# First mixer: the order of projections, attention heads, convolution taps and gates in the row of work behind the delta rule

## The chip, the cores and the metric

The kernel runs on one core of a Trainium2 chip. The metric is the time of one execution on the device, in microseconds (us). A trace comes from one profiled execution: its span runs from the first instruction to the last.

## What is computed

Two blocks stand one behind the other. The first has two layers, each a hybrid mixer and a feed-forward part; the second is other code that the change does not touch. For the change only the hybrid mixer matters. 256 tokens of width 1024 are projected once, and three branches share the result:

```python
def hybrid_mixer(x, w_in, mix_scale, w_out, ...):
    proj = jnp.einsum('btd,de->bte', x, w_in)
    (a_q, a_k, a_v, a_decay, a_beta, a_gate, c_glu, f_q, f_k, f_v, f_forget) = split_columns(proj, IN_SIZES)
    ...
    o_a = gated_delta_rule(heads(a_q, GDN_HEADS), heads(a_k, GDN_HEADS), heads(a_v, GDN_HEADS), log_decay, beta)
    o_a = (rms_norm_f32(o_a, gdn_norm_w) * jax.nn.silu(heads(a_gate, GDN_HEADS))).reshape(B, T, GDN_WIDTH)

    glu_a, glu_b = jnp.split(c_glu, 2, axis=-1)
    u = glu_a * jax.nn.sigmoid(glu_b)
    u = causal_depthwise_conv(u, cnv_dw_w) + cnv_dw_b          # 31 taps, 256 channels
    o_b = jax.nn.silu(layer_norm(u, cnv_ln_g, cnv_ln_b))

    log_f = jax.nn.log_sigmoid(f_forget + fox_f_bias)
    o_c = forgetting_attention(heads(f_q, FOX_HEADS), heads(f_k, FOX_HEADS), heads(f_v, FOX_HEADS), log_f)   # 6 heads

    mixed = jnp.concatenate([o_a, o_b, o_c], axis=-1) * mix_scale
    return jnp.einsum('bte,ed->btd', mixed, w_out)
```

All weights and activations are 32-bit floats.

## The kernel before, in words

Activations lie with the channels on the 128 partitions and the 256 tokens along the free axis. Weights come as one stream in the order of their use, in chunks of up to 1 MB ([128, 2048]) through four buffers `raw` (`load_chunk`, line 384). A projection takes its weights in one of two ways, set per group by `WHOLE` (line 165): with 'p' ScalarE and VectorE split each 1024 columns into a high and a low part (`hi`, `lo`, four buffers of each) and TensorE makes three matmuls per 128 x 128 piece (`mm3`); with 'w' one 32-bit matmul is made straight from `raw`, which shows as two records. A weight group accumulates in one PSUM bank of the tag `mm`, of which there are three.

`_mixer1` (line 727) is called once for each of the two layers. Its projections form one generator, `parts` (line 809), one step per call of `next`: the attention's values and the small columns, the delta rule's values v, then fq and fk of the attention (six steps, 'p'), gb and ga of the convolution (four steps each, 'w'), and the gates (two steps 'p', two steps 'w'). `fox` (line 1191) is the attention as a generator of ten steps: one that prepares the decay rows, then for each of three pairs of heads two steps of scores and softmax and one of the product with v. `conv_taps` (line 1166) is the convolution: a first step that starts both channel halves, then 30 steps of two VectorE instructions, `cvacc<-uu,cdwh,cvacc`, one behind the other in each half. It needs `uu`, which is made when ga is complete. `mem_load` (line 1600) loads the second block's memory and scales it by eight ScalarE instructions, and each `mem_units` (line 1610) makes a quarter of one layer's memory keys and values, 32 records of matmuls from a chunk of its own.

The delta rule (`gdn`, line 928) is a long chain of small matmuls and VectorE, ScalarE and GpSimd steps. Behind it `_mixer1` calls `fill(REST)` (line 871), which runs a row of such steps as a string spells it: c is a projection step, x a step of the attention, a digit that many steps of taps, U the memory load and u a memory unit. Steps that are asked for when a generator is at its end do nothing. Behind the row come the split of the attention's output into `mh`, `ml` (which take the buffers of the layer's input `xh`, `xl`, and so wait for the last 'p' projection), the convolution's layer norm (`conv_norm`, line 1179: squares, statistics on TensorE, the norm), one Silu over all gates (`G`), the gating and norm of the delta rule's output (`gdn_out`, line 1143), and the output projection w_out, which takes the attention's rows first, then the convolution's, then the delta rule's (`order = [5, 6, 7, 3, 4, 0, 1, 2]`, line 883 on).

The program's place is a priority and not yet the order of issue. When the program is built, a scheduler fills each engine's queue: of the instructions that its own clockwork holds ready it takes the one that stands first in the program, so work of the row goes into the gaps of the delta rule. Buffers of one tag are given out in the program's order. On the chip each queue runs in its order.

Of the kernel before, what the change touches and what calls it, by code (L numbers as in the profile page):

```python
# [160 lines left out]
FREE = 1  # L161
PRE = 2
FILL = ({'s': 'cccc', 'g': 'cccccc'}, {'s': 'cccc', 'g': 'cccccc'})
REST = 'ccccxccxcxcxcxcxcxcxcccx33x33U333c3c3c3cu999u'
WHOLE = ('wwwpppwwpw', 'pwwpppwwpw')
PG = 2
MO = 6
# [13 lines left out]
class K:  # L181
# [545 lines left out]
    def _mixer1(self, l, first):  # L727
# [94 lines left out]
        def fill(p):  # L822
            for n in p:
                if n == 'c':
                    next(stream, None)
                elif n == 'x':
                    next(box['fox'], None)
                elif n == 'U':
                    self.mem_load(f"m{l}")
                elif n == 'u':  # L830
                    if units:
                        self.mem_units(f"m{l}", [units.pop(0)])
                else:
                    for _ in range(int(n)):
                        next(conv, None)
# [34 lines left out]
        oS = self.gdn(l, qkv, lr, g, lnb, fill)  # L870
        fill(REST)
        mh, ml = self.new_hl()
# [1114 lines left out]
```

## Time and profile before

| | us |
|---|---|
| median of 3 runs | 2951.46 |
| lowest and highest | 2949.2 and 2954.4 |
| the profiled execution | 2954.75 |
| its span | 2952.9 |
| mean granted TensorE clock in it | 0.983 |

The profile's page gives each engine's busy time and groups the instructions by line. Since helpers record every operation (lines 202 to 217), a group is told by its tiles: `out<-in` names what an instruction writes and reads. In the trace layer 0's mixer is at 0 to 230 us and layer 1's at 420 to 640 us. gb and ga are `ps_mm<-x,raw`, taps are `cvacc<-uu,cdwh,cvacc`, the heads' scores are `ps_mm<-cr,selt`, `ps_mm<-selt,cr` and `ps_mm<-fb`, w_out and 'p' projections are `ps_mm<-xh,hi`, `xl,hi`, `xh,lo`, memory units are `ps_mm<-raw`. Matmuls are pipelined, so a busy TensorE need not be at its peak, and the start to start distance in a dense stream is its pace.

### The profile page before, as it was taken

The numbers are of one execution on the slowest core, as the hardware profiler recorded it, in microseconds if no ns is written. First come the engines' busy times: TensorE is split into PE (matmuls) and PEld (weight loads), VectorE is DVE, ScalarE is ACT, GpSimd is POOL, SyncE is SP. The second block draws the span as 40 slices with busy tenths as digits, with TensorE's granted clock in tenths as the row PEclk, the third lists the DMA queues.
The fourth block names the chain that finished last, engine by engine and source line by source line (L and its number), as shares of the span: only waits on it lengthen the run. The fifth ranks groups of instructions, "written<-read, shape, count | busy, mean of one in ns | idle before, by whom it ended". The sixth has DMA issues, their size and how long they took to land.

```text
span 2952.9 us, 48784 instructions
## 1 busy us (share of the span) xinstructions
PE 2894.1 (98%) x19525; PEld 2628.7 (89%) x19525; DVE 2155.8 (73%) x3156; ACT 1754.5 (59%) x2582; POOL 79.8 (3%) x142
## 2 busy tenths in 40 slices
PE   8999999999999999999999999999999999999998
PEld 7889998887888887788878899989999999999998
DVE  6476566479989888988889866676766665867764
ACT  5335445258787777778777744565554444655543
POOL 1100002000000000000000000100000000100000
PEclk9899999899999999999999999999999999999999
DMA  6035542158989997998999755534655555335553
GB/s 226 22 136 186 188 151 99 38 225 350 345 339 358 362 359 296 361 353 331 357 368 357 275 175 188 177 108 158 211 188 192 184 191 193 137 110 194 203 189 112
DMA packets 104205, 663.77 MB, mean 225 GB/s; under 512 B 11808, under 2 KB 17952, under 8 KB 28576
## 3 DMA queue, kind: packets, MB, share of 16 engines
q1 hardware_dynamic: 101664, 658.46, 60.6%
q8 instruction: 156, 2.56, 0.3%
q10 hardware_dynamic: 2304, 2.10, 0.2%
q14 instruction: 81, 0.66, 0.1%
HBM read 657.36 MB, written 3.15 MB: 224 GB/s over the span
## 4 chain that ended last, share of the span: by engine, by line
PE 57%; DVE 2%; ACT 1%; issue 0%; POOL 0%; POOLq 0%; DVEq 0%; ACTq 0%
PE ps_mm L217 47%; PE py L217 5%; PE ps_fx L217 2%; PE ps_sm L217 2%; DVE lo L206 1%; PE ps_fx L227 0%; PE ps_sm L227 0%; DVE aa L1784 0%; ACT hi L202 0%; DVE gi L206 0%; PE ps_st L217 0%; DVE aa L206 0%; ACT xr L203 0%; DVE y L214 0%; DVE ffab L206 0%
## 5 line engine op out<-in xcount | busy, mean ns | idle before, releaser
L206 DVE TENSOR_TENSOR lo<-raw,hi 128x1024 fp32r<-128x1024 f32 (+2 forms) x1216 | 1434.3, 1207 | 384.2 <-ACT hi L202 371.8
L202 ACT ACTIVATE hi<-raw 128x1024 fp32r<-128x1024 f32 (+2 forms) x1216 | 1246.8, 1044 | 622.0 <-PE ps_mm L217 466.7
L217 PE MATMUL ps_mm<-xh,hi 128*128 128x256 f32 x2736 | 777.1, 285 | 13.1 <-ACT hi L202 8.1
L217 PE MATMUL ps_mm<-xh,lo 128*128 128x256 f32 x2736 | 770.2, 282 | 2.1 <-DVE lo L206 2.1
L217 PE MATMUL ps_mm<-xl,hi 128*128 128x256 f32 x2736 | 771.8, 282 | 0.3 <-DVE xl L206 0.3
L217 PEld LDWEIGHTS ps_mm<-xh,hi 128*128 128x128 f32 x2736 | 519.5, 190 | 19.7 <-ACT hi L202 8.8
L217 PEld LDWEIGHTS ps_mm<-xh,lo 128*128 128x128 f32 x2736 | 518.6, 190 | 5.7 <-issue 2.7
L217 PEld LDWEIGHTS ps_mm<-xl,hi 128*128 128x128 f32 x2736 | 520.5, 190 | 3.5 <-issue 2.0
L217 PE MATMUL ps_mm<-lo,xgh 128*128 128x512 f32 x896 | 356.5, 398 | 0.7
L217 PE MATMUL ps_mm<-hi,xgl 128*128 128x512 f32 x896 | 349.8, 391 | 0.0
L217 PE MATMUL ps_mm<-hi,xgh 128*128 128x512 f32 x896 | 349.6, 392 | 0.0
L217 PE MATMUL ps_mm<-ffl,hi 128*128 128x256 f32 x880 | 245.6, 279 | 0.0
L217 PE MATMUL ps_mm<-ffh,hi 128*128 128x256 f32 x880 | 245.6, 279 | 0.0
L217 PE MATMUL ps_mm<-ffh,lo 128*128 128x256 f32 x880 | 245.5, 279 | 0.0
L217 PEld LDWEIGHTS ps_mm<-lo,xgh 128*128 128x128 f32 x896 | 168.4, 188 | 48.4 <-DVE lo L206 16.3
L217 PEld LDWEIGHTS ps_mm<-hi,xgh 128*128 128x128 f32 x896 | 168.5, 188 | 35.6 <-ACT hi L202 0.2
L217 PEld LDWEIGHTS ps_mm<-hi,xgl 128*128 128x128 f32 x896 | 168.6, 188 | 32.5
L217 PE MATMUL py<-lo,hh 128*128 128x512 f32 x448 | 178.5, 398 | 0.5
L217 PE MATMUL py<-hi,hl 128*128 128x512 f32 x448 | 174.8, 392 | 0.5
L217 PEld LDWEIGHTS ps_mm<-ffl,hi 128*128 128x128 f32 x880 | 165.4, 188 | 0.0
L217 PEld LDWEIGHTS ps_mm<-ffh,lo 128*128 128x128 f32 x880 | 165.4, 188 | 0.0
L217 PEld LDWEIGHTS ps_mm<-ffh,hi 128*128 128x128 f32 x880 | 165.4, 188 | 0.0
(433 smaller groups left out, 3735.7 us busy)
## 6 DMA issues: line engine op xcount, KB each, us to landing
raw<-in_sm SPq DMA_DIRECT2D x336, 1024.0 KB, 6.9
raw<-in_s SPq DMA_DIRECT2D x248, 1024.0 KB, 4.8
raw<-in_s SPq DMA_DIRECT2D x40, 512.0 KB, 3.3
raw<-in_s SPq DMA_DIRECT2D x32, 256.0 KB, 2.9
raw<-in_mem SPq DMA_DIRECT2D x5, 1024.0 KB, 4.9
kv<-kvt ACTq DMA_DIRECT2D x16, 128.0 KB, 5.4
raw<-kv SPq DMA_DIRECT2D x16, 128.0 KB, 2.8
raw<-in_s SPq DMA_DIRECT2D x2, 1005.0 KB, 6.7
```

The source lines that it names most:

```text
L202: return self.nc.scalar.activation(out, in_, func, scale=scale, **kw)
L206: return self.nc.vector.tensor_tensor(out=out, in0=a, in1=b, op=op)
L217: return self.nc.tensor.matmul(out, lhsT=l, rhs=r, start=start, stop=stop, skip_group_check=True, **kw)
```

## The change

One string is replaced; no step is added or left out (the last digits of both strings ask for more taps than are left).

```diff
-REST = 'ccccxccxcxcxcxcxcxcxcccx33x33U333c3c3c3cu999u'
+REST = 'ccccccxcccccccc3x3x3x3Ux3ux3x3x3x3xcccc3u9'
```

Written out, with H0 to H5 for the scores of the six heads, PV0 to PV2 for the products with v and tN for the taps up to step N (31 is the last):

```text
before: fq fq fq/fk fq/fk prep fk fk H0 gb H1 gb PV0 gb H2 gb H3 ga PV1 ga H4 ga ga gate
        H5 t3 t6 PV2 t9 t12 U t15 t18 t21 gate t24 gate t27 gate t30 - u t31 u
after:  fq fq fq/fk fq/fk fk fk prep gb gb gb gb ga ga ga ga t3 H0 t6 H1 t9 PV0 t12 U
        H2 t15 u H3 t18 PV1 t21 H4 t24 H5 t27 PV2 gate gate gate gate t30 u t31
```

The row is the same for both layers. The order in which weights stand in the stream follows the order of the loads.

## Rows read from the trace of the kernel before

**Rows 1.** the page, busy times: engine, us, share of the span, instructions
```profile
PE 2894.1 (98%) x19525; PEld 2628.7 (89%) x19525; DVE 2155.8 (73%) x3156; ACT 1754.5 (59%) x2582; POOL 79.8 (3%) x142
```

**Rows 2.** windows: length; busy us of PE, PEld, DVE, ACT, POOL; clock; DMA
```profile
84.00:126.00 42.00, 41.65 (x235) 35.12 (x235) 15.64 (x37) 13.42 (x42) 3.29 (x2) 0.80 0.00 1
126.00:157.00 31.00, 31.00 (x235) 24.39 (x234) 8.83 (x32) 11.22 (x32) 0.00 (x0) 1.00 0.10 35
157.00:184.00 27.00, 27.00 (x157) 23.77 (x155) 26.91 (x73) 8.39 (x18) 0.00 (x0) 1.00 0.39 127
```

**Rows 3.** windows of tile x, PE alone (gb, ga): length, busy us (records), clock
```profile
84.00:126.00 42.00, 10.19 (x26) 0.80 0.00 1
126.00:157.00 31.00, 10.31 (x38) 1.00 0.10 35
...
494.00:530.00 36.00, 6.98 (x24) 0.70 0.00 0
530.00:574.00 44.00, 12.19 (x40) 0.90 0.07 25
```

**Rows 4.** timeline of VectorE, layer 0: start us, us, instruction, idle before
```profile
156.81 0.75 DVE L214 SCALAR_TENSOR_TENSOR uu<-fb,ps_mm 128x256 f32<-128x256 f32 x2 [1.56 <-PE ps_mm L217]
...
164.06 18.17 DVE L214 SCALAR_TENSOR_TENSOR cvacc<-uu,cdwh,cvacc 128x249 f32<-128x249 f32 x48
...
186.72 1.23 DVE L206 TENSOR_TENSOR lo<-raw,hi 128x1024 fp32r<-128x1024 f32 x1
...
198.64 0.88 DVE L214 SCALAR_TENSOR_TENSOR xl<-G,pc,xh 128x256 fp32r<-128x256 f32 x2
```

**Rows 5.** lines of PE in 157 to 184: busy us, mean ns
```profile
L217 PE MATMUL ps_mm<-raw 128*128 128x256 f32 x64 | 14.0, 379 | 0.0
```

**Rows 6.** windows behind the taps, both layers, columns as in rows 2
```profile
184.00:217.50 33.50, 31.26 (x251) 29.74 (x250) 22.70 (x48) 14.76 (x25) 3.35 (x3) 0.95 0.52 197
601.00:627.00 26.00, 24.09 (x207) 23.05 (x206) 16.79 (x32) 14.21 (x23) 4.25 (x3) 1.00 0.64 237
```

**Rows 7.** timeline of PE, layer 0, columns as in rows 4
```profile
192.04 0.28 PE L217 MATMUL ps_mm<-xh,hi 128*128 128x256 f32 x1
...
193.34 0.28 PE L217 MATMUL ps_mm<-xh,lo 128*128 128x256 f32 x1
193.64 1.14 PE L217 MATMUL ps_sm<-cst,ovr 128*64 128x128 f32 x12
```

**Rows 8.** lines of PE in 84 to 126: busy us, mean ns
```profile
L217 PE MATMUL ps_mm<-fb 64*128 64x128 f32 (+1 forms) x12 | 3.5, 375 | 0.0
...
L217 PE MATMUL ps_mm<-cr,selt 128*128 128x256 f32 x6 | 2.2, 364 | 0.0
```

**Rows 9.** timeline of ScalarE, layer 0, columns as in rows 4
```profile
182.22 2.00 ACT L202 ACTIVATE hi<-raw 128x1024 fp32r<-128x1024 f32 x2 [4.16 <-DMA raw<-in_s]
184.13 0.40 ACT L203 ACTIVATE sq<-cvacc 128x256 f32<-128x256 f32 x1
...
195.25 1.28 ACT L203 ACT_TABLE_LOAD   x1
196.54 1.27 ACT L203 ACTIVATE G<-G 128x1280 f32<-128x1280 f32 x1
```

**Rows 10.** loads: the page's DMA group, and the timeline of SP and ScalarE
```profile
raw<-in_s SPq DMA_DIRECT2D x248, 1024.0 KB, 4.8
...
66.00 0.33 SPq L1605 DMA_DIRECT2D raw<-in_mem  x1
...
72.44 2.50 ACT L202 ACTIVATE raw<-raw,pc 128x256 f32<-128x256 f32 x6
```

**Rows 11.** windows: the half clock of layer 1; equal work of both layers
```profile
508.26:538.98 30.72, 30.72 (x129) 27.18 (x130) 6.40 (x13) 7.46 (x21) 1.64 (x1) 0.50 0.00 1
...
84.20:156.80 72.60, 72.25 (x465) 59.12 (x464) 24.07 (x67) 24.63 (x74) 3.29 (x2) 0.88 0.05 16
493.50:574.10 80.60, 80.60 (x468) 66.20 (x467) 26.28 (x76) 24.61 (x74) 5.31 (x5) 0.81 0.04 14
```

## What the change should do to the time: the prediction

> **What bounds the kernel now.** I read the page's busy times first, then the two mixers cut into stretches, then three queues in order of time. The page has TensorE at 2894.1 of 2952.9 us [rows 1], so nothing is won by making another engine faster, only by giving TensorE less to wait for or a better clock. The first mixer runs twice, once per layer. In layer 0 the delta rule runs to about 151 us (its last state product is evicted at 150.07), and TensorE is full in all of 84 to 184 us [rows 2]: the scheduler orders by place in the program but lets whatever is ready go ahead, so the pieces of the row REST already sit in the delta rule's gaps. What TensorE does there is fixed work. The change can't remove it; it can only shorten what comes after, or alter the clock under it.
>
> The place where the order matters is the convolution. Its two projections (gb, ga) are 64 matmul records per layer. In layer 0, 26 fall before 126 us and 38 in 126 to 157; in layer 1, 24 before 530 and 40 by 574 [rows 3]. The last lets `uu` start at 156.81, and the taps then fill VectorE: 48 of them take 18.17 us, 0.379 each, up to 182 us [rows 4]; VectorE is busy 26.91 of 27 us in that stretch [rows 2]. All that time TensorE still has work, 14.0 us of it the two units of memory keys and values [rows 5]. So the taps are late, but TensorE comes to the output projection (w_out) only at 184 us: the taps end about when it does. What is lost stands behind: 184 to 217.5 us holds 251 matmuls in 33.5 us, and in layer 1 601 to 627 holds 207 in 26 us [rows 6]. The pace of w_out at the full clock is 11 steps from 192.04 to 193.34, 0.118 us each [rows 7]. 251 and 207 at that pace are 29.6 and 24.4 us, so 3.9 and 1.6 us are lost, 5.5 together. The 59 and 63 of these that are not w_out's are small and go faster: twelve of them take 1.14 us at 193.64 [rows 7], 0.095 each, which makes 1.4 us more lost in each layer, 8.3 in all.
>
> **The change, part by part.** Nothing is added or taken away: 18 projection steps, 10 attention steps, 31 tap steps, the memory load U and its two units stay, each with the same instructions. Four things move.
>
> (1) gb and ga ahead of the heads. In the gaps before 126 us the heads now take score matmuls of 3.5 and 2.2 us [rows 8], products of 2.4 us and three smaller kinds of 1.6, 1.4 and 1.4 us (the same view); 12.5 us in all. At the 10.19 us that 26 records took there [rows 3], 0.39 each, they hold 32 more. So 58 of 64 are done by 126 and all by about 130 us; in layer 1, by the same count, about 532 instead of 574. TensorE's total is unchanged: 0. Bounds: the same records cost 0.39 there and 0.27 later (10.31 us for 38), but the heads leave that slow stretch in exchange, so I put plus or minus 2 us per layer for the exchange.
>
> (2) Taps between the heads. They start at about 130, need 62 x 0.379 = 23.5 us of VectorE, which in 126 to 157 is busy 8.83 of 31 us [rows 2], and so end near 164 instead of 182. What they meet is the delta rule's own VectorE steps between 126 and 150 (four gram products, three of `qg`, three of `vn`, three groups for the state: 13), each held up by at most one tap, 0.38 us: 0 to 5 us per layer on that chain. TensorE waits for it only if it has nothing else; heads and the first memory unit are ready there. I count 0.5 per layer, 1 us in all, 10 at the upper end.
>
> (3) What is late next. The convolution's statistics stand behind the whole row, and the second memory unit is in the row, so TensorE still takes them up only when the row is empty, near 183 us. So the chain does not move up by 18 us. It gets shorter. Now ScalarE does two weight splits from 182.22 before it squares the taps' sums, the first at 184.13 [rows 9], the second at 185.49 behind a memory unit's eviction; with taps done at 164 both squares are ready, which takes about 1.5 us out. VectorE puts splits of 1.23 us between the steps of the layer norm (186.72 and another behind it) [rows 4]: in layer 0 2.4 us, in layer 1 nothing. From the first statistics at 183.6 to the end of the second operand of the convolution at 199.5 is 15.9 us now; 12.0 then. What TensorE has to put under it is w_out of the attention's three rows, 54 matmuls at 0.118 (6.4 us), and 59 small ones (5.6 us): 12.0. It just covers. So layer 0 keeps about 0.5 of its 3.9 to 5.3 us and layer 1 about 0.5 of its 1.6 to 3.0: a gain of 4.5 to 7.3. I take 6.5, near the end that prices small matmuls by their own pace. Bounds: 0 if the cover fails by the same amount as now, 8.3 if all is recovered.
>
> (4) The gates go last, and the loads go in another order. U and the first unit now stand ahead of the gates, so the four buffers hold gb, ga, memory, unit; the gates' chunk waits for gb's buffer (about 105 us) instead of landing before U, which now issues at 66.00 [rows 10]. A chunk lands 4.8 us after its issue [rows 10] and its two splits take 2 x (1.00 + 1.23) us [rows 4, 9]; it is needed after the heads, behind 150, so I count 0, and 9.3 us per layer if that cover were gone. U's eight scalings (0.42 us each [rows 10], 3.3 us of ScalarE) move forward beside the first decay; the projections' dense stream covers them: 0, or 3.3. The gates' last result must pass table load and Silu (1.28 + 1.27 us [rows 9]), gating and split, about 7.4 us; the second unit (7 us) and w_out's first 6.4 us lie over it: 0.
>
> Sum: -6.5 + 1 and, for the clock, -0.5 (below): -6. Against the profiled execution (2954.75 us, of which 2952.9 is span) that is 2948.7; the median of the runs lies 3.3 us below that execution, so 2945.5 there, which I round to 2945.
>
> **The clock.** TensorE was granted 0.50 (1.2 of 2.4 GHz) in 508.26 to 538.98, with no idle time in it. Nearly the same work (84.20 to 156.80 and 493.50 to 574.10) took 72.6 and 80.6 us at 0.88 and 0.81 [rows 11]. With only 1.0 and 0.5 granted, 0.88 over 72.6 us is 17 us of half clock, so layer 1 had 13.6 us more of it and took 8.0 us longer: 0.6 us per us. In these stretches TensorE was busy with the inverse's small matmuls and one filling item between them. The change swaps those items, attention for projections, and the stretch can come out longer or shorter; I see no reason for a sign beyond layer 1's being the longer, and count -0.5, with -8 to +16 as ends (layer 1 like layer 0; each layer one more stretch of 13.6).
> The Trainium skill, "TensorE: Matmul & The Clock Gate", section "HAM oscillation — how this bites in real kernels", puts the lower clock down to gaps in which TensorE is idle. By that, an order that leaves it no gaps costs and gains nothing in clock, and the third and fourth case below would have no chance. The stretch with 30.72 busy of 30.72 at 0.50 speaks against it here.
>
> **The rivals.**
> A (0.46): as summed, 2942 to 2948, two thirds of it below 2945.6.
> B (0.23): the tail doesn't shorten. The statistics still wait for the row, the splits of w_out's weights still fall into the layer norm's steps (their buffers come free late, with the gates behind), and the gates' Silu takes the taps' place. For it: in layer 1 no split sits between the norm's steps and 1.6 us are lost even so. Against it: the squares no longer wait. Price 0 to 2: 2949 to 2953.
> C (0.15): slower. The projections are used up at about 130, so the rest of the delta rule has only heads and one unit as filling, and the half clock comes back or lasts: from one more 13.6 us in each layer on, 16 us less the 6: 2961; with one of them 2953. It decides once the half clock of the two mixers exceeds its present 48 us by more than 20.
> D (0.16): faster still. More matmuls of 256 columns early end the half clock sooner; layer 1 like layer 0 gives 8 on top of 6: 2937, and 2932 with layer 0 shorter too.
> That the scheduler gives much the same order as before is the lower end of B; the moved buffers speak against it.
>
> **How the numbers follow.** A measurement of this kernel tells 0.2%, 5.9 us, from no change. Faster: two thirds of A and D, 0.46. Same: the rest of A and B, 0.39. Slower: C, 0.15. The range 2932 to 2957 leaves out some of D's lower end and the greater part of C.
>
> **What would show it.** In the new profile: gb and ga complete by about 130 and 532 us; taps end by 165 and 580; the convolution's squares stand directly behind them; the stretch from the first statistics to w_out's end is 4 to 5 us shorter in layer 0 and about 2 in layer 1; TensorE stays full from 84 to 184. Wrong would be: holes in TensorE between 130 and 184, statistics later than 184, or a half clock of other length that outweighs the tail.

## The result and the profile after

The changed kernel takes 2973.5 us (median of 5, 2966.6 to 2974.2) against 2951.5 before: a ratio of 1.0068 [1.0054, 1.0083], slower by some 20 us. The profiled execution spans 2972.0 us at a mean granted clock of 0.979; before, 2952.9 at 0.983.

Executions of one and the same kernel, on one chip, differ by up to 27 us here, and go with the mean granted clock: over all timed executions of this study one line with a common slope, 2.66 us for each 0.001 of clock, leaves a spread of only 1.6 us. So below each kernel has two numbers: its mean clock (uncertain by about 0.0007 for 12 executions), and how far it lies above the kernel before **at equal clock** (about 0.5 us).

The stretches of layer 0 after, in windows (columns as in [rows 2]: stretch, its length, busy us of PE, its weight loads, DVE, ACT and POOL, granted clock, DMA share, GB/s). The first is one stretch of half clock, the next three answer to [rows 2], the last runs from the first statistics to the end of the output projection [rows 6]:

```profile
91.35:122.07 30.72, 30.72 (x124) 27.41 (x124) 5.29 (x8) 7.98 (x24) 1.64 (x1) 0.50 0.04 7
84.00:126.00 42.00, 41.97 (x201) 37.00 (x199) 9.86 (x18) 11.44 (x35) 3.28 (x2) 0.63 0.07 25
126.00:157.00 31.00, 29.96 (x213) 22.63 (x213) 14.66 (x40) 8.93 (x21) 0.00 (x0) 0.99 0.16 52
157.00:184.00 27.00, 27.00 (x159) 22.13 (x157) 21.95 (x69) 11.36 (x35) 0.00 (x0) 0.95 0.15 49
...
194.29:228.56 34.27, 30.26 (x254) 28.72 (x253) 20.75 (x46) 14.60 (x24) 3.35 (x3) 1.00 0.45 164
```

TensorE is as full as before, but at 0.63 in the first 42 us, and it comes to the statistics at 194.29 instead of 183.58. The last row is no shorter than before [rows 6]: 4.0 of 34.27 us without work.

The records of the convolution's projections, which answer to [rows 3]:

```profile
84.00:126.00 42.00, 15.71 (x38) 0.63 0.07 25
126.00:144.40 18.40, 7.45 (x26) 1.00 0.10 30
```

64 records, the last at 144.4. VectorE's timeline around the taps (start, duration, instruction, count; before: [rows 4]) shows `uu` at once behind them and the last taps at 187, not at 164:

```profile
144.38 0.75 DVE L214 SCALAR_TENSOR_TENSOR uu<-fb,ps_mm 128x256 f32<-128x256 f32 x2
145.05 0.41 DVE L211 TENSOR_SCALAR cvacc<-uu,cdwh,pc 128x256 f32<-128x256 f32 x1
...
185.78 1.18 DVE L214 SCALAR_TENSOR_TENSOR cvacc<-uu,cdwh,cvacc 128x227 f32<-128x227 f32 x3
```

ScalarE behind the taps, which answers to [rows 9]:

```profile
187.87 0.41 ACT L203 ACTIVATE sq<-cvacc 128x256 f32<-128x256 f32 x1
192.53 2.01 ACT L202 ACTIVATE hi<-raw 128x1024 fp32r<-128x1024 f32 x2 [4.26 <-DMA raw<-in_s]
194.50 0.39 ACT L202 ACTIVATE kvt<-ps_mm 128x256 f32<-128x256 f32 x1
...
195.57 0.41 ACT L203 ACTIVATE zq<-cvacc 128x256 f32<-128x256 f32 x1
...
201.39 1.06 ACT L202 ACTIVATE hi<-raw 128x1024 fp32r<-128x1024 f32 x1 [5.41 <-PE ps_mm L217]
```

The first square is directly behind the taps, but the second stands behind two weight splits that wait 4.26 us for their load, and behind the eviction of the second memory unit.

In layer 1 the half clock of the inverse is shorter than before (20.48 against 30.72 us [rows 11]), and the tail lies partly at half clock:

```profile
524.84:545.32 20.48, 20.48 (x84) 18.36 (x82) 4.02 (x6) 6.12 (x18) 0.00 (x0) 0.50 0.15 51
614.72:644.81 30.09, 26.79 (x207) 25.68 (x206) 16.31 (x32) 13.35 (x21) 4.26 (x3) 0.89 0.56 206
```

At the end of the output projection the changed kernel is 11.2 us late in layer 0 and 17.8 in layer 1. Of the 6.6 us between, 2.8 arise near 370 us, where TensorE has a stretch of half clock that the kernel before did not have and the code is unchanged; so layer 1's own mixer adds little in this execution.

### The profile page after: what moved, and what is told of

Read it like the earlier page. It is cut to its first block, busy times and chain, and to the rows that moved or that the text cites. A ratio compares the mean times of both kernels' runs of the same rounds, so it can differ in the third digit from the quotient of the medians.

```text
span 2972.0 us, 48789 instructions
## 1 busy us (share of the span) xinstructions
PE 2907.3 (98%) x19525; PEld 2637.2 (89%) x19525; DVE 2154.6 (72%) x3156; ACT 1753.6 (59%) x2582; POOL 76.3 (3%) x142
## 4 chain that ended last, share of the span: by engine, by line
PE 57%; DVE 2%; ACT 1%; issue 0%; POOL 0%; POOLq 0%; DVEq 0%; ACTq 0%
PE ps_mm L217 47%; PE py L217 5%; PE ps_fx L217 2%; PE ps_sm L217 2%; DVE lo L206 1%; PE ps_fx L227 0%; PE ps_sm L227 0%; DVE aa L1784 0%; ACT hi L202 0%; DVE gi L206 0%; PE ps_st L217 0%; DVE aa L206 0%; ACT xr L203 0%; DVE y L214 0%; DVE ffab L206 0%
## 5 line engine op out<-in xcount | busy, mean ns | idle before, releaser
L217 PEld LDWEIGHTS ps_mm<-hi,xgl 128*128 128x128 f32 x896 | 168.8, 188 | 32.5
```

Source lines behind the costliest of these rows:

```text
L217: return self.nc.tensor.matmul(out, lhsT=l, rhs=r, start=start, stop=stop, skip_group_check=True, **kw)
```

## The experiments

All runs at a glance. The medians of the kernel before in the four batches were 2956.5, 2951.5, 2952.9 and 2954.1, its mean clock over 124 executions 0.9839 (0.9830, 0.9848, 0.9840 and 0.9838 in the batches of e1 to e4, of a2 and e5 to e7, of e8 to e11, and of e12 to e15). Behind a run stand 12 executions, but 11 behind a2_after, 9 behind e12_tiny, 6 behind e10 and e11, and 5 behind the first.

| run | median us | ratio to before | mean clock | at equal clock, us |
|---|---|---|---|---|
| changed kernel, first | 2973.5 | 1.0068 [1.0054, 1.0083] | 0.9798 | +7.5 |
| a2_after (the same again) | 2973.7 | 1.0061 [1.0038, 1.0083] | 0.9803 | +8.2 |
| e1_layer0 | 2963.5 | 1.0032 [1.0015, 1.0049] | 0.9814 | +4.4 |
| e2_layer1 | 2955.4 | 1.0004 [0.9988, 1.0021] | 0.9843 | +3.6 |
| e3_taps_behind | 2958.4 | 1.0010 [0.9994, 1.0027] | 0.9846 | +6.5 |
| e4_heads_front | 2954.5 | 0.9988 [0.9964, 1.0012] | 0.9856 | +3.8 |
| e11_units_old | 2978.9 | 1.0083 [1.0051, 1.0114] | 0.9808 | +15.2 |
| e5_unit_behind | 2962.2 | 1.0036 [1.0016, 1.0056] | 0.9825 | +4.2 |
| e7_old_unit_behind | 2957.8 | 1.0019 [0.9997, 1.0040] | 0.9834 | +1.7 |
| e12_tiny (new row, 16 x 16 columns) | 2968.3 | 1.0048 [1.0029, 1.0066] | 0.9826 | +10.4 |
| e13_cols256 (new row, 16 x 256) | 2954.1 | 1.0001 [0.9985, 1.0018] | 0.9879 | +11.1 |
| e6_dense (new row, 16 x 512) | 2953.0 | 1.0004 [0.9990, 1.0019] | 0.9892 | +13.5 |
| e15_old_tiny (old row, 16 x 16) | 2970.6 | 1.0051 [1.0033, 1.0069] | 0.9788 | +2.8 |
| e14_old_cols256 (old row, 16 x 256) | 2947.1 | 0.9974 [0.9960, 0.9988] | 0.9885 | +5.7 |
| e8_old_dense16 (old row, 16 x 512) | 2950.3 | 0.9993 [0.9976, 1.0010] | 0.9872 | +5.6 |
| e9_old_dense8 (old row, 8 x 512) | 2955.4 | 0.9998 [0.9979, 1.0017] | 0.9857 | +4.9 |
| e10_old_dense4 (old row, 4 x 512) | 2985.4 | 1.0103 [1.0075, 1.0130] | 0.9752 | +5.7 |

**Is the lower clock the change's?** The changed kernel was run again beside others.

> The changed kernel once more, beside the others of its batch. The executions of one kernel spread by about 25 us, and go with the mean granted clock of the execution at about 2.65 us for each 0.001. Theory P (part and part): the change costs 7 to 8 us at equal clock, and the other 12 of the first comparison were a lower clock in its five executions (0.980 against 0.983 to 0.986); if that was chance, its mean clock is now like that of the kernel before, and it stands 6 to 10 us above it. Rival K: the longer half clock belongs to the new order; then its mean clock is again 0.003 or more below that of the kernel before and it stands 15 to 20 us above.

Eleven executions, 2956.5 to 2978.8 at 0.986 to 0.977, mean clock 0.9803: K's case. So about 8 us are there at equal clock, and 0.0038 of clock, times 2.66 us for each 0.001, is 10: together the 18 us by which the mean of all 16 executions lies above that of the kernel before (the medians differ by 20 to 22). What one stretch of half clock costs is seen where two executions run the same 134 matmuls of layer 0's inverse, first in a2_after, then in e1_layer0 (windows, columns as above):

```profile
88.12:116.65 28.53, 28.53 (x134) 26.77 (x134) 3.92 (x6) 5.40 (x14) 3.27 (x2) 0.56 0.00 1
```
```profile
87.89:105.41 17.52, 17.52 (x134) 15.91 (x134) 3.92 (x6) 5.21 (x14) 3.28 (x2) 1.00 0.00 1
```

At 0.56, 25.1 of the 28.53 us are half clock; they cost 11.0 us, 0.44 each. The common slope says the same: 0.001 of mean clock over 2954 us is 5.9 us of half clock, and 2.66 over 5.9 is 0.45 (an estimate). The order of instructions alone doesn't decide it: TensorE's order up to the end of layer 0's mixer is the same in these two executions, and ran once at half, once at full clock. What the order shifts is the mean.

**Layer by layer.** The old and the new row as two strings, one per layer:

```
-        fill(REST)
+        fill(REST[l])          # e1: (new, old), e2: (old, new)
```

> The new row in layer 0 alone, the old row in layer 1. Theory K (clock): what the change costs comes mostly from the longer half clock in layer 0's delta rule (34 us of it against 17) and from what it does to the granted clock afterwards; so layer 0 ends its mixer 9 to 12 us later than in the kernel before, and the whole is 2961 to 2967. Rival O (order): each layer loses alike because heads and taps stand in one another's way, about 10 us per layer; then also about 2961, but the loss shows in a stretch at the full clock, between 145 and 195 us, and the layer 1 kernel of this batch loses as much.

> The old row in layer 0, the new row in layer 1 alone. Theory K: in the changed kernel layer 1 had 20.5 us of half clock in the delta rule against 30.7 and won 5 us there, lost some 3 in the row and 4 in the tail; alone it gives 2949 to 2955, and the time goes with the half clock of its own trace at 0.5 us per us. Rival O: each layer loses about 10 us by its order; 2961.

At equal clock +4.4 and +3.6 add up to the +8 of both: each layer loses alike, though not the 10 us that O gave it. The lower clock goes with layer 0, as K had it: beside 0.9830 for the kernel before in the same batch, the new row there alone has 0.9814, in layer 1 alone 0.9843. But -0.0016 and +0.0014 do not add up to the -0.0038 of both, so it isn't shown that layer 0 alone brings the loss of clock. (The profiled execution of e1 happens to have no half clock in layer 0's inverse and ends that mixer at 214.84, earlier than before, so its trace doesn't show K's 9 to 12 us.) The two profiled executions also make a pair that is nearly free of the clock: in layer 0 both have 0.98 up to the statistics and 1.00 behind them. (e2 has 3.4 us of half clock near 44 us as well, which makes it 1.7 us late at the last matmul that both orders have in common; so the pair is measured from that matmul on.) First e2 (old row), then e1 (new row), up to the statistics and from there to the end of the output projection:

```profile
69.32:178.73 109.41, 108.47 (x720) 89.99 (x718) 65.78 (x174) 38.84 (x107) 15.18 (x12) 0.98 0.15 54
178.73:211.10 32.37, 30.21 (x254) 28.71 (x252) 23.11 (x48) 15.08 (x25) 3.35 (x3) 1.00 0.54 204
```
```profile
67.62:180.51 112.89, 111.05 (x719) 90.45 (x718) 67.27 (x176) 35.95 (x100) 13.24 (x12) 0.98 0.17 62
180.51:214.84 34.33, 30.35 (x254) 28.82 (x253) 20.57 (x46) 14.46 (x24) 3.34 (x3) 1.00 0.45 163
```

The new row takes 3.5 us longer to its statistics (112.89 against 109.41; 0.9 of that is time without work), and its tail is 2.0 us longer, with the same 254 matmuls and 1.8 us more without work. In layer 1 the tails, both at full clock, are 26.0 us in e1 (old row) and 27.4 in e2 (new row).

**Which of the moves?** Projections in front, but all heads ahead of the taps, and gates, load and units where they stood:

```
-REST = 'ccccccxcccccccc3x3x3x3Ux3ux3x3x3x3xcccc3u9'
+REST = 'ccccccxccccccccxxxxxxxxx3333U333c3c3c3cu999u'
```

> Both layers: the convolution's projections in front as in the change, but all heads ahead of the taps and the gates, memory load and units where they stood before. Theory K: the delta rule gets the same filling as in the changed kernel, so the half clock of layer 0 stays at 30 us or more, and the time stays at 2965 to 2975. Rival O, in the form that the taps between the heads cost the time: the loss goes, 2948 to 2955.

Neither as put. At equal clock nearly the whole loss stays (+6.5), so the projections in front are enough to bring it, without the taps between the heads; but the clock is not lower than that of the kernel before (0.9846). K's reason, that projections in place of heads make the filling of the inverse too light, is not borne out: e3 has projections there too, and a mean clock over 12 executions that is no lower (in its profiled execution the inverse of layer 0 ran at full clock).

Heads among the projections as before, with only the gates last and the load and units early:

```
+REST = 'ccccxccxcxcxcxcxcxcxcc3x33x3U333u33333cccc3u9'
```

> Both layers: the heads among the projections as before the change, the projections of the convolution no earlier than before; only the gates go last and the memory load and units stand earlier, as in the change. Theory K: the filling of the delta rule is the old one, so its half clock in layer 0 is 17 us again and the time is 2948 to 2956. Rival L (loads): the gates last and the memory chunks moved past them cost the time, by late weights or buffers; then 2960 or more with the old clock.

The clock is not lower (0.9856), as K had it, and the time the same as before within the interval; at equal clock it costs 3.8 us, with layer 1's tail as before (25.9 us at full clock; layer 0's holds half clock), so the gates and loads are not free. Where in the row these 3.8 us lie was not separated.

Taps between the heads, with gates, load and units back in their old places:

```
-REST = 'ccccccxcccccccc3x3x3x3Ux3ux3x3x3x3xcccc3u9'
+REST = 'ccccccxcccccccc3x3x3x3x3x3x3x3x3x3U3c3c3c3cu999u'
```

> The changed kernel with the memory load, the two units and the gates back in the places that they had before, so that of the change there stay the projections in front and the taps between the heads. With all heads ahead of the taps the like kernel gave a mean clock of 0.985 and cost 6.6 us at equal clock. Theory T (the taps between the heads bring the lower clock): mean clock 0.980 to 0.982, 14 to 20 us above the kernel before. Rival G (the units, the load and the gates do): mean clock 0.984 to 0.986, 3 to 9 us above.

The low clock of T (0.9808), at a price that neither had: +15.2 at equal clock. From e3_taps_behind this row differs only in where the taps stand, so there the taps between the heads bring the clock from 0.9846 down to 0.9808; by what path is not shown. The row of its layer 0, from the delta rule's end to the statistics:

```profile
141.60:188.67 47.07, 42.93 (x209) 33.64 (x209) 28.64 (x82) 15.63 (x43) 0.00 (x0) 0.82 0.18 65
```

Against full windows before [rows 2] TensorE has no work for 4.1 us here, and for 4.6 in layer 1 (565 to 620.18): three times in each it waits for a head's exponentials on ScalarE (`fp`), and both units, which could fill the holes, come at the end. That the softmax is late because it takes turns with the taps on VectorE is argued. In this execution some 17 us of half clock fall into that very stretch (0.82 over 47.07 us). So with taps between the heads the early unit, load and late gates of the change were a help; which of the three was not separated.

**Does the tail wait for the second unit?** It is emitted behind the norm of the convolution, in the changed kernel and in the one before:

```
+REST = '...cccc39'             # e5; e7: the old row without its last u
         self.conv_norm(l, G)
+        fill('u')
```

> The changed kernel with one step moved: the second memory unit is emitted behind the convolution's norm instead of before its last taps. Theory S: in the changed kernel the taps end 7 us before TensorE has finished that unit, and the statistics, with the chain to the output projection behind them, wait for it; with the unit behind them the chain starts up to 7 us earlier, and the unit fills the holes of the tail (4.0 us idle in layer 0, 3.3 in layer 1), so 4 to 8 us come back at equal clock, and the time at equal clock is that of the kernel before within 4. Rival W: the tail waits for weights of the output projection whose buffers the unit holds; then the unit behind the statistics makes these later still, and the time is that of the changed kernel or up to 5 us more.

> The row of the kernel before with only the second memory unit moved behind the convolution's norm. Theory S: there the taps end 1.3 us before TensorE comes to the statistics, so nothing waits for the unit; the tail's idle 2.2 and 1.9 us can be filled in part: 0 to 3 us less at equal clock. Rival W: the output projection's weights come later: 1 to 4 us more.

S holds for the new row, at the low end of its range: 4 us come back at equal clock (+4.2 instead of +8.2). Its profile, from the delta rule's end to the statistics and on to the end of the output projection:

```profile
147.75:180.52 32.77, 32.26 (x185) 26.59 (x186) 26.95 (x83) 14.28 (x44) 0.00 (x0) 0.95 0.11 41
180.52:218.33 37.81, 35.81 (x282) 33.82 (x281) 23.22 (x48) 16.13 (x26) 3.35 (x3) 1.00 0.55 202
```

The tail now contains most of the unit and has 2.0 us without work instead of 4.0. For the old row it is W's case, 1.7 us more: there the taps end only 1.35 us ahead of the statistics (182.23, 183.58), and nothing waited for the unit.

**What holds the clock up?** Added matmuls, one ahead of each group of small ones in the inverse, 16 per layer, overwritten by what follows. Between the three runs on the new row only their columns differ, not their places:

```
+    def dense(self):
+        ps = self.bank("sm", shape=(4, 128))
+        self.mm(ps, self.identb, self.masks["mL"][:, None, :].to_broadcast([128, 4, 128]), start=True, stop=True)
+        return ps
...
-                    px = self.bank("sm", shape=(3, 128))
+                    px = self.dense()[:, :3]      # likewise the banks pz and pd
```

> The changed kernel with 16 more matmuls of 512 columns per layer, one ahead of each group of small matmuls in the inverse of the delta rule; their result is overwritten. At the full clock they are 0.22 us each, 3.5 us per layer. Theory K: the half clock comes from the inverse's small matmuls and lighter filling; with the added columns its stretches in the two inverses shrink to 10 us or less each, the mean clock rises by 0.004 or more, and the time falls by 4 to 10 us in spite of the 7 us of work. Rival: the clock does not depend on it; then the time rises by 4 to 7 at the same mean clock.

> The changed kernel with 16 added matmuls per layer as in the run with 512 columns each, in the same places, but of 16 columns. Theory K (columns in the inverse hold the clock up): mean clock as in the changed kernel, 0.978 to 0.982; 18 to 28 us above the kernel before. Rival D (the other order of the fillers did it): mean clock 0.986 to 0.990, and the time 0 to 6 us above the kernel before.

> The changed kernel with the same 16 added matmuls per layer of 256 columns each. Theory K: mean clock between 0.982 and 0.989, between the control with 16 columns and the run with 512. Rival D: 0.986 to 0.990 like the one with 512 and like the control.

In the new row the mean clock goes 0.9826, 0.9879, 0.9892 with 16, 256 and 512 columns, and the time 2968, 2954, 2953 in spite of the added work. The inverse of layer 0 in the three profiled executions, with 16, then 256, then 512 columns:

```profile
88.28:118.17 29.89, 29.89 (x146) 27.31 (x145) 3.92 (x6) 5.37 (x14) 3.27 (x2) 0.56 0.00 1
```
```profile
89.57:108.46 18.89, 18.88 (x144) 17.22 (x143) 3.92 (x6) 5.41 (x14) 3.28 (x2) 0.91 0.00 1
```
```profile
89.69:111.11 21.42, 21.42 (x144) 18.74 (x142) 3.92 (x6) 5.41 (x14) 3.28 (x2) 0.84 0.00 1
```

TensorE shows next to no idle time in any of them, and yet the clock differs. In the first two, TensorE's records from the first to the last small product of the inverse are the same 126 in the same order; they take 27.1 us with 16 columns and 16.8 with 256. One execution decides little, but the mean clocks (0.9826 and 0.9879, each uncertain by less than 0.001) go the same way. So in the new row the added columns raise the clock: K's case, against D, though the control with 16 columns lies just above K's range for it (0.978 to 0.982), and the gain of 512 columns beside the changed kernel (20 us) is twice the most that K put.

The same on the old row, with fewer of them as well:

> The kernel before, with 16 added matmuls of 512 columns per layer in the delta rule's inverse, as they were added to the changed kernel. There they cost 5 us at equal clock and lifted the mean clock from 0.980 to 0.989. Theory K: the half clock follows from the inverse's small matmuls whatever the row is; the mean clock rises from 0.984 to 0.989, worth 12 to 14 us, the work costs 5: 5 to 10 us below the kernel before. Rival N (the new order alone makes the clock fall): the old order has nothing to win, 3 to 6 us above.

> The kernel before, with 8 of the added matmuls per layer (ahead of the two groups of small products, not ahead of the transposes). Theory K: half the work, 2 to 3 us, and the greater part of the clock: 4 to 10 us below. Rival N: 1 to 3 us above.

> The kernel before, with 4 of the added matmuls per layer. Theory K: 1 us of work and a part of the clock: 0 to 6 us below, with a mean clock between that of the kernel before and that with 8. Rival N: 0 to 2 us above.

> The kernel before with 16 added matmuls per layer of 256 columns each. Theory K: about half of the work that 512 columns cost (2 to 3 us at equal clock) and a mean clock of 0.985 to 0.988: 0 to 6 us below the kernel before. Rival D: the clock of the control with 16 columns.

> The kernel before with 16 added matmuls per layer of 16 columns each. Theory K: mean clock 0.982 to 0.985, like the kernel before, 0 to 5 us above it. Rival D: away from it, up to 0.988 or down to 0.976, as four added matmuls of 512 columns moved it.

With 16 columns the clock falls to 0.9788, with 256 and 512 it rises to 0.9885 and 0.9872: columns count here too. But the first of these, and the four of 512 columns (0.9752), lie 0.005 and 0.009 below the kernel before, while in the new row the 16 of 16 columns lie above the changed kernel (0.9826 against 0.9803). So added matmuls alone also move the clock, either way; that they do it by shifting the filling, as D has it, is argued. K's gains fail on the old row with 512 columns: sixteen bring 2.6 us instead of 5 to 10, eight cost 2.5 instead of bringing 4 to 10, and four cost 32.5 instead of bringing 0 to 6. Single executions don't carry the comparison: in layer 1 the inverse of e15 ran at 0.56 and that of e14 at 1.00 (the first pair), in layer 0 that of e15 at 0.76 and that of e14 at 0.62 (the second). The filling differs as well: in layer 0's inverse 10 records of gb and ga with 16 columns, 6 with 256.

```profile
515.25:545.21 29.96, 29.96 (x156) 27.09 (x154) 3.92 (x6) 5.75 (x14) 3.28 (x2) 0.56 0.00 1
```
```profile
515.28:535.17 19.89, 19.78 (x158) 17.29 (x157) 4.63 (x9) 6.22 (x17) 3.29 (x2) 1.00 0.00 1
```
```profile
93.24:117.73 24.49, 24.49 (x158) 22.00 (x157) 5.00 (x11) 6.97 (x20) 3.28 (x2) 0.76 0.00 1
```
```profile
93.25:120.14 26.89, 26.89 (x148) 24.27 (x147) 4.91 (x11) 6.67 (x19) 3.28 (x2) 0.62 0.00 1
```

By its interval e14, the kernel before with 16 matmuls of 256 columns in each inverse, is slightly faster than the kernel before: 0.9974 [0.9960, 0.9988]. What it is in the inverse that the half clock goes with (its narrow products, its 24 transposes, or the evictions between them) no run separates.

## Why the prediction was wrong, step by step

**The clock** is the step that failed most. I counted -0.5 us and saw no reason for a sign; it is +10 (0.0038 of mean clock over 16 executions of the changed kernel), inside my bounds of -8 to +16 but taken at the wrong place. The price, 0.6 us per us of half clock from [rows 11], was too high: 0.44 by the pair of inverses. What I missed is that one execution of each layer says little: the same 144 matmuls of layer 0's inverse took 24.88 us at 0.71 in the kernel before and 19.78 at 0.91 in e2_layer1. (Layer 1's half clock was the longer one in six of the ten profiled executions without added matmuls, so it isn't shown to have been chance alone.) Rival C had the mechanism's name and sign, and its highest time, 2961, still fell 12 us short. Its place was wrong, by the profiled execution: the half clock does not come back when the projections are used up; it begins at 91.35, while they are the filling. And its threshold, 20 us more of half clock, rested on a gain of 6 us that was not there: at equal clock the change is slower already. Of my own signs of being wrong, statistics later than 184 came true (194.29).

The Trainium skill, "TensorE: Matmul & The Clock Gate", section "HAM oscillation — how this bites in real kernels", traces the lower clock to idle gaps. Here the measurement decides against it as the only cause: columns added to stretches without idle time raised the mean clock, from 0.9826 (e12_tiny) to 0.9879 (e13_cols256). The Trainium skill, the same page, "Part 1: The HAM clock gate", notes that the number of slow matmuls at the start of one kernel changes from run to run. Here it is the mean over the whole kernel that changes, from 0.977 to 0.986 over eleven executions of a2_after.

**(1) The projections.** "All by about 130 us": 144.4 in the profiled execution at half clock, but `uu` is done at 131.5 in e1_layer0, where the inverse ran at full clock. In layer 0 the count was right, the clock under it not. In layer 1, for which I had 532, `uu` was done at 563.2 in the changed kernel and at 544.4 in e2_layer1, both with half clock in the inverse; no trace of the new row without added matmuls shows that count at the full clock. "TensorE's total unchanged, plus or minus 2 per layer" is not borne out: in layer 0 the new row takes 3.5 us more to the statistics, 0.9 of it new time without work (1.84 against 0.94).

**(2) The taps.** From `uu` to the last tap I gave 34 us; in e1_layer0 they took 41.7 (131.5 to 173.2), in the changed kernel 42. I had counted the delta rule's VectorE steps as what they meet, and not those of the heads, between which they now stand: the maxima, sums and scalings of the softmaxes. In these 41.7 us VectorE works 32.4 and waits 9.3, of which 6.1 are for the softmaxes' exponentials on ScalarE; the taps behind such a step in its queue wait with it.

**(3) The tail** was to get 6.5 us shorter and got 3.4 longer (2.0 and 1.4). I had let the bounds end at 0, without a reason that excluded a loss. Right was that the statistics wait for the whole row. Wrong was "both squares are ready": the second comes 8 us behind the first, behind splits and evictions in ScalarE's order. But TensorE did not wait for it: it takes that square's sums at 197.27, 1.3 us after the square is done, behind 14 steps of w_out.

What failed is "it just covers". I counted all 54 matmuls of the attention's rows of w_out as work to put under the norm. In the old row (e2_layer1) TensorE's queue has 38 of them ahead of the norm's first small product and all 54 ahead of the last small product; in the new row (e1_layer0) 22 and 45, so behind the last one 147 of w_out's 192 steps are left, against 138. In the new row TensorE then waits for `ln_r` although the weights of the next steps of w_out were split by 176.5. And since these steps come later, they give the buffers of split weights back later: the sixth split starts 15.1 us behind the first statistics (195.60 against 180.51), where it starts 9.5 behind in e2_layer1 (188.23 against 178.73). On ScalarE it now stands ahead of the convolution's operand `xh<-G`. First e1_layer0 (new row), then e2_layer1 (old row):

```profile
192.22 1.27 ACT L203 ACTIVATE G<-G 128x1280 f32<-128x1280 f32 x1
195.60 1.06 ACT L202 ACTIVATE hi<-raw 128x1024 fp32r<-128x1024 f32 x1 [2.11 <-PE ps_mm L217]
196.57 0.89 ACT L202 ACTIVATE xh<-G,pc 128x256 fp32r<-128x256 f32 x2
```
```profile
191.59 1.27 ACT L203 ACTIVATE G<-G 128x1280 f32<-128x1280 f32 x1
192.89 0.91 ACT L202 ACTIVATE xh<-G,pc 128x256 fp32r<-128x256 f32 x2
```

The operand starts 3.1 us behind the Silu's end, where in the old row it followed at once. TensorE's waits in e1_layer0:

```profile
185.63 0.71 PE L217 MATMUL ps_sm<-cst,ln_r 128*128 128x128 f32 x4 [0.58 <-POOL ln_r L525]
...
197.11 0.62 PE L217 MATMUL ps_mm<-xh,hi 128*128 128x256 f32 x3 [0.73 <-ACT xh L202]
198.37 0.39 PE L217 MATMUL ps_mm<-xl,hi 128*128 128x256 f32 x1 [0.64 <-DVE xl L214]
```

Of these 1.95 us the old row has only a wait of 0.31 for `xl`; that is 1.6 of the 1.8 us that layer 0's tail has more without work. The tail of layer 0 is as long, 34.2 us at full clock, in e3_taps_behind and e11_units_old, whose gates and units stand as before: so it comes with the projections in front. Why the scheduler then sets the small products earlier among the steps of w_out stays open. The unit behind the statistics (e5_unit_behind) brings 4 us back.

**(4) Gates last and loads** counted at 0 cost 3.8 us at equal clock when made alone (e4_heads_front), with a tail of 25.9 us at full clock in layer 1, as before. My bound of 9.3 per layer held; the value was not supported by any row.

So without the clock the change would still have been 8 us slower, where I had 6 faster: rival B's place (the tail doesn't shorten) with a price above its 0 to 2, and the rows' own loss on top. These 8 us don't split exactly: gates and loads alone cost 3.8, projections in front without them 6.5, both together 8.2.

What stays open is why one order meets the half clock more often than another: e3_taps_behind has the projections in front and no lower clock, and e15_old_tiny the old row and a clock lower than the change's.

## What to carry to other kernels

Where a chain of small matmuls is filled with whatever is ready, a new order of the fillers can change TensorE's granted clock by an amount that a single trace of the kernel before does not foretell; time such a change over ten or more executions, and compare at equal mean clock, or the order is blamed for the clock and the clock for the order. Before counting a chain as shorter because its input is ready earlier, list what stands ahead of each of its steps on each engine: here a weight split that waited for a buffer stood on ScalarE ahead of an operand that could have started 3 us earlier, and small products stood on TensorE ahead of large ones that were ready. If a stretch of small matmuls sits at half clock although TensorE is full, wide matmuls added to it can be worth a try: sixteen of 256 columns won 0.26% on the old row, but four of 512 lost 1.0%.

## What was not expected of the hardware

The same 134 matmuls took 17.52 us at a granted clock of 1.00 and 28.53 at 0.56, both without a hole in TensorE's records. One kernel's executions spread over 22 us (2956.5 to 2978.8, a2_after) as their mean clock went from 0.986 to 0.977. Sixteen added matmuls per layer of 256 columns raised the mean clock from the 0.9788 of their 16-column control to 0.9885 in the old row, and from 0.9826 to 0.9879 in the new one; four of 512 columns in the old row lowered it from 0.9839 to 0.9752.
